# Delta rule in a hybrid encoder block: one head's first phase a piece later, one filler piece moved from step 8 to step 3

## The chip, the cores and the metric

The kernel runs on one core of a Trainium2 chip. The metric is the time of one execution on the device, in microseconds; a kernel's time is the median of several executions. Beside these runs one more execution was taken with the hardware profiler on; all lines of a profile below come from that one.

Engines are named as the profile names them: PE is TensorE (matmuls), PEld its weight loads, DVE is VectorE, ACT is ScalarE, POOL is GpSimd, SP is SyncE, which here issues DMAs. Each engine works through its own queue in order.

## The reference

The reference is one layer of a bidirectional encoder block on 256 tokens of 2048 channels. From a normalized and modulated input it computes one large projection, whose columns feed two branches: an mLSTM (branch A, 4 heads) and a gated delta rule (branch B, 16 heads of 128), each run forwards and backwards over the sequence. Both are projected back, merged by gates and added to the input; a SwiGLU feed-forward part follows. The change touches the schedule of branch B:

```python
qkv = jax.nn.silu(centred_depthwise_conv(b_qkv, gdn_conv_w))
q_b = l2_normalize(heads(b_q, B_HEADS, B_DK)) * (B_DK ** -0.5)
k_b = l2_normalize(heads(b_k, B_HEADS, B_DK))
...
a_mat = jnp.eye(CHUNK) + betac[..., :, None] * jnp.einsum('nbhid,nbhjd->nbhij', kc, kc) * decay_strict
t_mat = lax.linalg.triangular_solve(a_mat, jnp.broadcast_to(jnp.eye(CHUNK), a_mat.shape),
                                    left_side=True, lower=True, unit_diagonal=True)
u = jnp.einsum('nbhij,nbhje->nbhie', t_mat, betac[..., None] * vc)
w = jnp.einsum('nbhij,nbhjd->nbhid', t_mat, (betac * jnp.exp(gc))[..., None] * kc)
...
v_new = u_ - jnp.einsum('bhid,bhde->bhie', w_, s_mem)
o = jnp.einsum('bhid,bhde->bhie', q_ * jnp.exp(g_)[..., None], s_mem) + jnp.einsum('bhij,bhje->bhie', attn, v_new)
s_mem = jnp.exp(g_last) * s_mem + jnp.einsum('bhjd,bhje->bhde', k_ * jnp.exp(g_last - g_), v_new)
```

The modulation (shift, scale, gate) is a matrix-vector product with a weight of 6 x 2048 rows.

## The kernel before

**Heads, groups and pairs.** The 16 delta heads form four groups of four (`GRP = 4`). Each group g goes through an inversion of small triangular blocks (`gdn_invert`, `gdn_blocks`), and then its heads are worked on in two pairs, p = 0 (the "first pair") and p = 1 (the "second pair"), by `gdn_phase2(g, p)`. Phase 2 is a generator of nine steps; each step is a few matmuls and the copies behind them, and each step's matmuls need the copies of the step before. In the trace their PSUM tiles are called p (steps 1 to 4, lines 830, 839, 852 and 864), pa (step 5), pb (step 6), pc (step 7), po (step 8) and px (step 9).

**Pieces between the steps.** So that PE has work while it would wait for a step's copies, pieces of large projections are put between the steps. Those come from `stream(h0)`, line 956: for the two heads h0 and h0+1 of the group after, three jobs `b_job(h, j)` (the columns of k, q and v), each of two pieces. A piece of a `b_job` is 8 blocks of three 128x256 matmuls (the weights are split into a high and a low part: `wh` by ACT, `wl` by DVE), and the last piece of a job ends in `gdn_conv`: ACT copies the result into a padded tile, a depthwise conv follows (one step on ACT, four on DVE, line 351), and a silu on ACT (line 354) writes into kq or vf. That silu is put off (the list `behind`) and emitted with the next job's piece. When the 12 pieces of the two heads are out, `stream` takes further pieces from the list `fills` (other projections).

**Phase 1 inside the stream.** Six pieces after a head's first, all three of its columns are there, and `stream` notes two entries in `todo` for it: the first half of `gdn_phase1(h)` runs behind the second piece from then, its second half behind the fourth. The first half has four scans on DVE, splits of k and q (`kqh`, `kql`), squares (`sqkq`), and on PE two transposes of vf and eight one-column matmuls into `vps`; the second half has six matmuls into two `ks` tiles, some 16 DVE instructions that read them, and DMAs on POOL: four into `inst_d`, one back into `uu` for the next inversion, and `decay_load(h + 2)`. So the pair's first head has its halves behind pieces 8 and 10, and the second behind 14 and 16, where the stream of a pair ends.

**The counts.** The main loop runs steps n = 1 to 9, and behind each step as many pieces as a tuple says: `after` for first pairs, `second` for second pairs of groups 0 to 2, `last` for both pairs of group 3, for which there are no further heads. Counting up `after` gives 1, 3, 4, 6, 8, 10, 12, 16 pieces behind steps 1 to 8, and `second` gives 2, 4, 5, 7, 9, 11, 13, 16. In first pairs, steps 1 to 4 also advance `gdn_blocks`, which copies blocks out of `cg` into X (steps 1 and 2) and UL (steps 3 and 4; line 813 on DVE, line 815 on ACT).

**The modulation rows.** `pump()`, line 159, is called in each piece. It keeps one 1 MB row of the modulation weight in flight (tile `ada`, loaded through SyncE) and, when a row has been there for three calls, emits its product and sum on DVE (line 125). The flag `held` keeps it from doing so in steps 1 to 3 of a pair.

**Order.** The code's order is a priority. A planner in the framework orders each engine's queue by it with a model of times, and can pull an instruction ahead where its model sees the engine free; only what is wrapped in `order(...)` keeps program order on its engine.

Of the kernel before, what the change touches and what calls it, by code (L numbers as in the profile page):

```python
# [25 lines left out]
GRP = 4  # L26
# [26 lines left out]
def hybrid_block(ctx: ExitStack, tc: tile.TileContext, xr, nfr, crow, pk_d, cst_d, ada2, ada4, win0, winb, wint, wba, wbb, wo, wgu, wd, out, dbg=None):  # L53
# [228 lines left out]
    def fill(n=1):  # L282

        while n and fills:
            if next(fills[0], None):
                n -= 1
            else:
                fills.pop(0)
# [103 lines left out]
    def b_job(h, j):  # L392
        return fjob(f"b{h}_{j}", winb[3 * (h - GRP) + j], lambda ps: gdn_conv(h, j, ps))
# [562 lines left out]
    def stream(h0):  # L956

        todo = []

        def piece():  # L960

            for q in list(todo):
                q[0] -= 1
                if not q[0]:
                    todo.remove(q)
                    next(heads1[q[1]])

        for h in range(h0, min(h0 + 2, NH_B)):
            for j in range(3):
                for _ in b_job(h, j):  # L970
                    piece()
                    yield True
            todo += [[2, h], [4, h]]
        while todo:
            fill(1)
            piece()
            yield True
        while True:
            fill(1)
            yield True  # L980
# [94 lines left out]
        yield  # L1075

    heads1 = {h: gdn_phase1(h) for h in range(NH_B)}
    after = (0, 1, 2, 1, 2, 2, 2, 2, 4, 0)
    last = (0, 1, 2, 1, 2, 2, 1, 1, 3, 0)
    second = (0, 2, 2, 1, 2, 2, 2, 2, 3, 0)  # L1080

# [21 lines left out]
    for g in range(4):  # L1103
# [15 lines left out]
        for p in range(2):  # L1119
            pieces = stream(4 * g + 2 * p + 4)  # L1120
            for n in range(1, 10):

                held[0] = n < 4
                if p == 0:
                    next(blocks, None)
                next(pairs[p], None)
                if g == 3 and n == (8, 4)[p]:
                    next(first2[p])
                for _ in range(last[n] if g == 3 else second[n] if p else after[n]):
                    next(pieces)  # L1130
            for _ in pairs[p]:
                pass

            if g < 3:
                while 4 * g + 2 * p + 5 not in heads:
                    next(pieces)
# [577 lines left out]
```

## Time and profile before

| what | value |
|---|---|
| median of 3 runs | 1943.1 us |
| lowest and highest run | 1942.42 and 1946.88 us |
| the profiled execution | 1947.25 us |
| its span from first to last instruction | 1945.5 us |
| granted TensorE clock, mean over the span | 0.998 |

The span is what the profile's shares refer to. In a list of groups or a timeline a line has the start (timeline only), the busy time, the engine, the source line, the operation, and "out<-in" with the names of tiles, then the number of instructions; "[0.76 <-ACT vf L354]" means that the engine stood idle for 0.76 us before it, until ACT finished writing vf at line 354. In a table of stretches, a number in brackets is a count of instructions. Matmuls are pipelined and their ends are modelled: two of them can overlap in the listing.

### The profile page before, as it was taken

To read this page: it belongs to the slowest core of one execution; us is meant where nothing else is said; L and a number is where in the kernel's file an instruction comes from. 1 tells how busy PE (TensorE), PEld (TensorE's weight loads), DVE (VectorE), ACT (ScalarE), POOL (GpSimd) and SP (SyncE) were. 2 spreads that over 40 slices of the span, in tenths; PEclk is the share of its full clock that TensorE was granted. 3 is DMA by queue.
4 is the path that set the end of the run, shared out by engine and by line. 5 is a ranking of instruction groups with operands and counts; after the bars stand their busy time and mean duration, and the time that the engine had idled before them with its cause. 6 is when DMAs were issued, how large, how long until landed. Compare 5 with 4: busy or idle time off the path is not lost.

```text
span 1945.5 us, 27233 instructions
## 1 busy us (share of the span) xinstructions
PE 1916.4 (99%) x10448; PEld 1700.4 (87%) x10448; DVE 1407.1 (72%) x2087; ACT 1028.0 (53%) x1562; POOL 124.1 (6%) x223
## 2 busy tenths in 40 slices
PE   8999999999999999999999999999999999999997
PEld 6888889998999899889788888888888888888886
DVE  6788886888888789866577888766666565555554
ACT  3147646775776587565544445644444444444443
POOL 0001220111011101120100000200000000000000
PEclk9999999999999999999999999999999999999999
DMA  9997676667676766686787898576777665565663
GB/s 398 420 360 243 181 258 249 216 221 238 219 231 205 235 225 238 208 286 244 252 307 262 352 349 321 195 260 244 248 250 252 238 221 204 203 208 203 199 211 131
DMA packets 80772, 485.67 MB, mean 250 GB/s; under 512 B 11433, under 2 KB 17137, under 8 KB 26625
## 3 DMA queue, kind: packets, MB, share of 16 engines
q1 hardware_dynamic: 64368, 451.02, 64.2%
q0 software_dynamic: 8672, 17.88, 4.4%
q10 hardware_dynamic: 7602, 15.03, 2.0%
q8 instruction: 82, 1.34, 0.3%
q14 instruction: 48, 0.39, 0.1%
HBM read 467.07 MB, written 16.82 MB: 249 GB/s over the span
## 4 chain that ended last, share of the span: by engine, by line
PE 86%; DMA 6%; DVE 5%; ACT 2%; issue 1%; POOL 0%; SPq 0%; DVEq 0%; ACTq 0%; POOLq 0%
PE acc_up L247 4%; PE acc_up L248 4%; PE acc_up L249 4%; PE acc_gt L248 4%; PE acc_d L248 4%; PE acc_gt L249 4%; PE acc_d L247 4%; PE acc_d L249 4%; PE acc_gt L247 4%; DMA ra<-ada 3%; PE acc_b L186 3%; PE acc_o L247 3%; PE acc_o L248 3%; PE acc_o L249 3%; PE acc_b L187 3%; PE acc_b L188 3%
## 5 line engine op out<-in xcount | busy, mean ns | idle before, releaser
L215 DVE TENSOR_TENSOR wl_d<-raw_d,wh_d 128x1024 fp32r<-128x1024 f32 x88 | 107.7, 1225 | 105.9 <-ACT wh_d L213 105.9
L215 DVE TENSOR_TENSOR wl_up<-raw_up,wh_up 128x1024 fp32r<-128x1024 f32 x88 | 107.7, 1225 | 100.7 <-ACT wh_up L213 100.7
L215 DVE TENSOR_TENSOR wl_gt<-raw_gt,wh_gt 128x1024 fp32r<-128x1024 f32 x88 | 107.7, 1224 | 76.9 <-ACT wh_gt L213 76.9
L186 PE MATMUL acc_b<-hh,wh_b 128*128 128x256 f32 x576 | 162.0, 281 | 0.0
L213 ACT ACTIVATE wh_d<-raw_d 128x1024 fp32r<-128x1024 f32 x88 | 92.9, 1056 | 126.8 <-PE acc_d L248 118.0
L188 PE MATMUL acc_b<-hh,wl_b 128*128 128x256 f32 x576 | 158.6, 276 | 0.0
L187 PE MATMUL acc_b<-hl,wh_b 128*128 128x256 f32 x576 | 158.5, 275 | 0.0
L213 ACT ACTIVATE wh_gt<-raw_gt 128x1024 fp32r<-128x1024 f32 x88 | 92.9, 1056 | 121.7 <-PE acc_gt L248 75.7
L213 ACT ACTIVATE wh_up<-raw_up 128x1024 fp32r<-128x1024 f32 x88 | 92.8, 1056 | 108.0 <-PE acc_up L248 77.0
L125 DVE SCALAR_TENSOR_TENSOR ada<-ada,crow 128x2048 f32<-128x2048 f32 x64 | 146.3, 2286 | 0.0
L247 PE MATMUL acc_up<-wh_up,hfh 128*128 128x512 f32 x352 | 133.4, 379 | 0.0
L248 PE MATMUL acc_up<-wh_up,hfl 128*128 128x512 f32 x352 | 133.4, 379 | 0.0
L249 PE MATMUL acc_up<-wl_up,hfh 128*128 128x512 f32 x352 | 133.4, 379 | 0.0
L247 PE MATMUL acc_gt<-wh_gt,hfh 128*128 128x512 f32 x344 | 131.6, 383 | 0.0
L248 PE MATMUL acc_gt<-wh_gt,hfl 128*128 128x512 f32 x344 | 130.5, 379 | 0.2 <-DVE hfl L1481 0.2
L248 PE MATMUL acc_d<-wh_d,ffl 128*128 128x512 f32 x344 | 130.5, 379 | 0.0
L249 PE MATMUL acc_gt<-wl_gt,hfh 128*128 128x512 f32 x344 | 130.4, 379 | 0.0
L247 PE MATMUL acc_d<-wh_d,ffh 128*128 128x512 f32 x344 | 130.4, 379 | 0.0
L249 PE MATMUL acc_d<-wl_d,ffh 128*128 128x512 f32 x344 | 130.4, 379 | 0.0
L603 PE MATMUL first<-x,raw 128*128 128x256 f32 x488 | 108.8, 382 | 6.4 <-ACT x L595 6.4
L603 PEld LDWEIGHTS first<-x,raw 128*128 128x128 f32 x488 | 91.6, 190 | 23.6 <-ACT x L595 11.6
L187 PEld LDWEIGHTS acc_b<-hl,wh_b 128*128 128x128 f32 x576 | 110.6, 192 | 0.1
(403 smaller groups left out, 5293.6 us busy)
## 6 DMA issues: line engine op xcount, KB each, us to landing
ada<-ada SPq DMA_DIRECT2D x64, 1024.0 KB, 5.3
raw_gt<-wgu SPq DMA_DIRECT2D x44, 1024.0 KB, 4.9
raw_up<-wgu SPq DMA_DIRECT2D x44, 1024.0 KB, 4.9
raw_d<-wd SPq DMA_DIRECT2D x44, 1024.0 KB, 4.9
raw_b<-winb SPq DMA_DIRECT2D x36, 1024.0 KB, 5.6
ra<-ada SPq DMA_DIRECT2D x30, 1025.0 KB, 15.1
raw_z<-wint SPq DMA_DIRECT2D x16, 1024.0 KB, 4.9
raw_v<-wint SPq DMA_DIRECT2D x16, 1024.0 KB, 5.9
```

Source lines behind the costliest of these rows:

```text
L125: order(V.scalar_tensor_tensor(raw, raw, 1.0, row_c[:, :D], ALU.mult, ALU.mult, accum_out=mod[:, c : c + 1]))
L186: PE.matmul(o, wh[:, k], woven(hh[:, kk]), start=kk == 0, stop=False)
L187: PE.matmul(o, wh[:, k], woven(hl[:, kk]), start=False, stop=False)
L188: PE.matmul(o, wl[:, k], woven(hh[:, kk]), start=False, stop=kk == KB - 1)
L213: order(S.activation(wh, raws[u][:, k0 : k0 + 2], AF.Copy), early)
L215: order(V.tensor_tensor(wl, raws[u][:, k0 : k0 + 2], wh.bitcast(F32), ALU.subtract), early or beside[0])
L247: order(PE.matmul(ps[t], xh[:, kk, c], woven(wh[:, k]), start=kk == 0, stop=False), early and steps > 1)
L248: PE.matmul(ps[t], xl[:, kk, c], woven(wh[:, k]), start=False, stop=False)
L249: PE.matmul(ps[t], xh[:, kk, c], woven(wl[:, k]), start=False, stop=kk == last)
L603: PE.matmul(first[o], raw[:, o], x[:, b], start=b == 0 and o % 2 == 0, stop=b == KB - 1 and o % 2 == 1)
```

## The change

Two tuples and two numbers change. For a head h with h % 4 = 2 (heads 6, 10 and 14: the first head of the stream in the second pairs of groups 0, 1 and 2), both halves of phase 1 run one piece later. In first pairs, two pieces in place of one stand behind step 3, and three in place of four behind step 8. The counts behind the steps of first pairs so become 1, 3, 5, 7, 9, 11, 13, 16.

```diff
@@ -970,7 +970,8 @@
                 for _ in b_job(h, j):
                     piece()
                     yield True
-            todo += [[2, h], [4, h]]
+            late = h % GRP == 2
+            todo += [[2 + late, h], [4 + late, h]]
         while todo:
             fill(1)
             piece()
@@ -1075,7 +1076,7 @@
         yield
 
     heads1 = {h: gdn_phase1(h) for h in range(NH_B)}
-    after = (0, 1, 2, 1, 2, 2, 2, 2, 4, 0)
+    after = (0, 1, 2, 2, 2, 2, 2, 2, 3, 0)
     last = (0, 1, 2, 1, 2, 2, 1, 1, 3, 0)
     second = (0, 2, 2, 1, 2, 2, 2, 2, 3, 0)
 
```

## The prediction

> **What bounds the kernel now.** I read the page first, for the engine that has no slack.
>
> ```profile
> span 1945.5 us, 27233 instructions
> PE 1916.4 (99%) x10448; PEld 1700.4 (87%) x10448; DVE 1407.1 (72%) x2087; ACT 1028.0 (53%) x1562; POOL 124.1 (6%) x223
> ```
>
> TensorE (PE) is busy 99% of the span. The edit adds no instruction and takes none away; it only moves work in time. So it can change the end in one way: by the time in which PE stands idle. I therefore asked for busy times by stretch, one stretch for each of the six pairs that the edit touches (two pairs in each of the groups 0, 1 and 2; lines in this order).
>
> ```profile
> core 0: us, PE busy (x) PEld busy (x) DVE busy (x) ACT busy (x) POOL busy (x), PEclk, DMA share, GB/s
> 314.60:373.00 58.40, 57.50 (x480) 56.11 (x478) 48.72 (x95) 44.13 (x92) 3.56 (x7) 1.00 0.67 221
> 373.00:432.00 59.00, 58.24 (x459) 55.99 (x458) 51.99 (x108) 42.97 (x90) 7.04 (x14) 1.00 0.69 221
> ...
> 494.60:552.10 57.50, 57.28 (x480) 56.07 (x478) 48.71 (x96) 44.27 (x91) 3.55 (x7) 1.00 0.67 228
> 552.10:611.00 58.90, 58.14 (x458) 55.93 (x457) 51.89 (x107) 42.88 (x90) 6.93 (x14) 1.00 0.69 221
> ...
> 672.30:729.70 57.40, 57.18 (x479) 55.93 (x477) 48.27 (x95) 44.95 (x89) 3.59 (x7) 1.00 0.66 218
> 729.70:789.00 59.30, 59.21 (x509) 58.13 (x509) 54.27 (x113) 44.43 (x93) 6.16 (x12) 1.00 0.68 228
> ```
>
> Length less PE's busy time is PE's idle time: 0.90, 0.22 and 0.22 us in the three first pairs, 0.76, 0.76 and 0.09 us in the three second pairs, together 2.95 us. This is all that the edit can win inside these pairs. Which waits these are is told by the list of waits of PE:
>
> ```profile
> engine line waited for: us in total, times, longest us
> ...
> PE acc_z L249 <- DVE wl_z L215: 1.8, 3, 0.7
> PE vps L674 <- ACT vf L354: 1.5, 2, 0.8
> PE acc_mb L249 <- DVE wl_mb L215: 1.3, 1, 1.3
> ...
> PE p L864 <- DVE pt L853: 0.7, 1, 0.7
> PE pb L888 <- DVE r L889: 0.4, 2, 0.2
> ...
> PE pa L877 <- DVE UL L813: 0.2, 1, 0.2
> ```
>
> The two vps waits are those of the second pairs of groups 0 and 1. The p and pa waits belong to the first pair of group 0, the two pb waits to the first pairs of groups 1 and 2. The other two rows lie outside the pairs.
>
> **How long a piece is.** In the second pair of group 1, PE starts a matmul of a projection job every 0.11 us; its modelled duration, 0.28, overlaps the next:
>
> ```profile
> 577.81 0.28 PE L187 MATMUL acc_b<-hl,wh_b 128*128 128x256 f32 x1
> 577.92 0.28 PE L188 MATMUL acc_b<-hh,wl_b 128*128 128x256 f32 x1
> 577.98 0.48 DVE L351 SCALAR_TENSOR_TENSOR cv<-pad,pk,cv 128x256 f32<-128x256 f32 x1
> ...
> 578.37 2.29 DVE L125 SCALAR_TENSOR_TENSOR ada<-ada,crow 128x2048 f32<-128x2048 f32 x1
> 578.49 0.42 ACT L354 ACTIVATE vf<-cv 128x256 f32<-128x256 f32 x1 [1.24 <-DVE cv L351]
> ...
> 578.96 0.44 PE L674 MATMUL vps<-cst,vf 128*128 128x128 f32 x2 [0.76 <-ACT vf L354]
> ```
>
> A b_job piece is 8 blocks of 3 matmuls, so 24 x 0.11 = 2.7 us. The rows also show the vps wait: the last of the four conv steps on VectorE (DVE) starts at 577.98, ScalarE's silu into vf starts at 578.49, and the transposes that read vf start at 578.96, 0.76 us late by the modelled end of the last matmul.
>
> **Part 1: the late head (h = 6, 10, 14).** Its first half (2 transposes and 8 one-column matmuls on PE, kqh and sqkq on ACT, kql and four scans on DVE) moves from behind piece 8 to behind piece 9, its second half from behind piece 10 to behind 11. Order on PE before: pa, piece 8, vps, piece 9, pb, piece 10, ks, piece 11, pc. After: pa, 8, 9, vps, pb, 10, 11, ks, pc. The vps comes 2.7 us later against a vf whose conv is not moved; 0.76 is less than 2.7, so both waits go and the third pair's 0.09 with them: -1.61. The moved second half also issues DMAs on POOL: four into inst_d, the one back into uu, and decay_load of head h+2. POOL is busy 6 to 7 us of 59 in these pairs and nothing is moved past another POOL instruction; uu is read only in the inversion, which still waits for the pair's last head (behind piece 16 as before), and the decay rows of h+2 are read a pair later or more. Cost 0. Without that slack it would be one piece, 2.7 us, each time. The SyncE queue isn't touched by this part.
>
> What is late next is pb, now right behind vps as it is in the first pairs. There its second half waits 0.22 us for r, because VectorE has put an ada row (2.29) in front:
>
> ```profile
> 519.76 2.28 DVE L125 SCALAR_TENSOR_TENSOR ada<-ada,crow 128x2048 f32<-128x2048 f32 x1
> ...
> 523.22 0.42 DVE L889 TENSOR_TENSOR r<-vv,pb 128x256 f32<-128x256 f32 x1
> ...
> 523.70 0.71 PE L888 MATMUL pb<-z,gg 128*128 128x128 f32 x4 [0.22 <-DVE r L889]
> ```
>
> The row can fall there in none or in all three: 0 to 0.66. I take 0.66, since the ada row is given out in the first piece of step 6 in both kinds of pair.
>
> **Part 2: one more piece behind step 3 of first pairs.** Steps 4 to 7 stand one piece later than before against pieces, conv and vps. In group 0 the wait goes that step 4 has for pt:
>
> ```profile
> 325.77 2.29 DVE L125 SCALAR_TENSOR_TENSOR ada<-ada,crow 128x2048 f32<-128x2048 f32 x1
> ...
> 328.38 0.69 DVE L853 TENSOR_TENSOR pt<-p,cst 128x512 f32<-128x512 f32 x1
> ...
> 329.12 0.43 PE L864 MATMUL p<-X,pt 128*128 128x64 f32 x2 [0.70 <-DVE pt L853]
> ```
>
> With 48 matmuls in place of 24, PE would come to step 4 about 2.7 us later, and 0.70 is covered. The pa wait of 0.2 goes likewise, since the UL copies that it waits for don't move. The pb of groups 1 and 2 comes a piece after vps, as in today's second pairs, where it shows no wait. Together -0.90 - 0.22 - 0.22 = -1.34.
>
> The held flag covers steps 1 to 3, so the first ada row is now given out in piece 6, then in 10 and 14, no longer in 5, 9 and 13. That is still three in 16 pieces, so none is left over for later. SyncE issues each ada load one piece later, behind one more raw load at most:
>
> ```profile
> ada<-ada SPq DMA_DIRECT2D x64, 1024.0 KB, 5.3
> ```
>
> From issue to landing takes 5.3 us, and a row's use is three pieces, 8 us, away: cost 0.
>
> What is late next is vf. From step 4 on the first pairs now have today's layout of second pairs: pa, piece 8, vps. And they have more to do there: the UL copies out of cg, which only first pairs have.
>
> ```profile
> 511.69 1.68 ACT L815 ACTIVATE UL<-cg 32x256 f32<-32x256 f32 x4
> ...
> 513.17 1.17 DVE L813 COPY UL<-cg 32x256 f32<-32x256 f32 x4
> ...
> 518.73 0.43 ACT L354 ACTIVATE vf<-cv 128x256 f32<-128x256 f32 x1
> ...
> 520.53 0.38 PE L674 MATMUL vps<-cst,vf 128*128 128x128 f32 x2
> ```
>
> Against pieces, vps itself isn't moved (behind piece 8 in both kernels), and today vf is ready 520.53 - 519.16 = 1.37 us before it. What eats this margin is the ada row, 2.29 us given out a piece later and so right before vf's conv, and the z copies of pa, which come later too. Lower bound of the new wait: 0, if VectorE, which has a backlog anyway, just does the same work in another order. Upper bound: the 0.76 of second pairs plus both copies, 0.76 + 1.17 + 1.68 = 3.6. I take 0.4, half of the second pairs' row, because total work ahead of vf is the same and only its order is worse: 3 x 0.4 = +1.2.
>
> **Part 3: one fewer behind step 8.** Three pieces, 8 us, stay between po and px; second pairs have three today and show no wait at px. Cost 0, and the pair still ends behind 16 pieces.
>
> **Sum.** -1.61 + 0.66 - 1.34 + 1.2 = -1.1 us. The profiled execution took 1947.25 us (span 1945.5), so it would be about 1946.1; that execution lies 4.1 above the median of 1943.1, and I carry the difference to the median: 1942.0.
>
> **The rivals.**
>
> First pairs wait for vf (the slower side). With w for the new wait in each first pair, the total is 3w + 0.66 - 2.95, so from w = 0.76, exactly today's wait of the second pairs, the kernel is slower than before. At the upper bound, 3.6, it is +8.5: 1951.6. For it speaks that the layout is one that waits today; against it the margin of 1.37 us. 0.3% is 5.8 us, about what a measurement of this kernel can tell from no change; that needs w = 2.7.
>
> [...] The trace's one dip in mid-kernel has this length, 3.40 us at 0.50, though PE has no idle time there:
>
> ```profile
> 946.40:949.80 3.40, 3.40 (x5) 1.35 (x4) 0.00 (x0) 1.63 (x2) 0.00 (x0) 0.50 0.98 336
> ```
>
> [...]
>
> All waits go: vf keeps its margin and pb never waits. -2.95, so 1940.1. For it: the margin. Against: in-order VectorE with the ada row in a worse place.
>
> The order doesn't come out as written. Not all instructions are held to program order; the ada row above starts at 578.37, before step 6, in whose first piece it is given out. If the planner puts vps, conv and ada where they were, nothing changes: 1943.1.
>
> Something outside the pairs moves: a planner that shifts by some us may order the inversion or later stages otherwise. The outside waits quoted (1.8 + 1.3), the dip (1.7) and the pairs (2.95) bound a gain at 7.8 us, 1935.3; there is no such bound for a loss.
>
> **How the numbers follow.** Forecast 0.43 (1942.0); vf wait 0.2, of which 0.08 above 5.8 us; all waits go 0.15; order unchanged 0.1; something outside 0.12, of which 0.07 is a gain over 0.3% and 0.05 a loss over it. So faster 0.07, slower 0.08 + 0.05 = 0.13, same 0.80. The range: 1938.8 to 1947.5. Its lower end is "all waits go" less the half microsecond or so by which the runs lie below their median; its upper end is w = 1.7, +2.8, plus some of the 3.8 us by which the highest run shown lies above the median.
>
> **What would show it.** In the changed profile: no vps wait in second pairs and no p L864 wait in the first pair of group 0 (parts 1 and 2 right); vps L674 <- ACT vf in first pairs, its length w (the term I am least sure of); pb L888 <- DVE r up to three times in second pairs; PE idle in the six stretches about 1.9 in place of 2.95. Wrong would be: idle time in a stretch above 3 us, a vps wait left in second pairs, another dip of the clock, or a change that lies outside 314 to 789 us.

## The result, and the profile after

The changed kernel takes 1951.33 us (median of 5 runs, 1950.75 to 1953.38), the kernel before 1943.96 us (5 runs, 1942.42 to 1946.88). The ratio is 1.0035, with a 95% interval of 1.0025 to 1.0046: by the ratio 6.8 us slower (the two medians differ by 7.4), a little over 0.3% and outside the predicted range. The profiled execution took 1953.38 us.

The page's top, after:

```profile
span 1951.5 us, 27218 instructions
PE 1921.3 (98%) x10448; PEld 1706.6 (87%) x10448; DVE 1408.5 (72%) x2087; ACT 1030.5 (53%) x1563; POOL 124.7 (6%) x223
```

PE has the same 10448 matmuls, but its busy time rose by 4.9 us, and ScalarE has one instruction more. Neither should happen in a pure reordering, and both are clues: matmuls took longer, and something was added to ScalarE.

Where the time came from is read by noting when PE starts step 1 (the first matmul of tile p) and step 9 (px) in both traces:

| stretch | before, us | after, us | difference |
|---|---|---|---|
| group 0, first pair (step 1 to step 1 of the second) | 58.31 | 60.12 | +1.81 |
| group 0, second pair (step 1 to step 9) | 57.61 | 57.45 | -0.16 |
| group 1, first pair | 57.41 | 57.39 | -0.02 |
| group 1, second pair | 57.61 | 57.44 | -0.17 |
| group 2, first pair | 57.42 | 58.01 | +0.59 |
| group 2, second pair | 57.42 | 61.48 | +4.06 |

The sum is 6.11 us, and the spans differ by 6.05; the rest of the kernel cancels out. Two places make the loss: the first pair of group 0, and the turn of group 2 from its first to its second pair. The same stretches as busy times (columns as in the prediction; group 0 first pair, group 2 both pairs):

```profile
314.40:374.60 60.20, 59.03 (x480) 57.68 (x478) 48.72 (x95) 44.23 (x92) 3.57 (x7) 0.97 0.63 214
...
673.90:731.90 58.00, 57.48 (x478) 55.88 (x476) 48.06 (x97) 45.63 (x91) 3.58 (x7) 1.00 0.65 229
731.90:795.30 63.40, 60.70 (x508) 59.69 (x509) 55.23 (x112) 46.31 (x95) 6.16 (x12) 0.97 0.63 209
```

Two of them have a granted clock of 0.97. Idle time alone (1.17, 0.52 and 2.70 us here) is less than the loss. PE's list of waits, after:

```profile
PE pb L888 <- DVE r L889: 1.9, 3, 0.8
PE acc_b L188 <- DVE wl_b L183: 1.2, 1, 1.2
...
PE vps L674 <- ACT vf L354: 1.2, 1, 1.2
PE p L839 <- DVE pt L831: 1.1, 1, 1.1
...
PE p L830 <- DVE at L719: 0.4, 1, 0.4
```

The second pairs' vps waits and the waits of step 4 and 5 in group 0 are gone, as forecast. New are a vps wait of 1.2 us in the first pair of group 0, three pb waits in the second pairs, and, in the turn of group 2, where the old kernel had none, waits in steps 1 and 2 and a wait of 1.2 us for wl_b in the piece behind them.

**The turn of group 2.** ScalarE's timeline there, before:

```profile
719.49 1.28 ACT L931 ACT_TABLE_LOAD   x1
720.79 0.30 ACT L931 ACTIVATE so<-so,epsc 128x4 f32<-128x4 f32 x1
720.99 1.04 ACT L181 ACTIVATE wh_a<-raw_a 128x1024 fp32r<-128x1024 f32 x1
722.05 1.28 ACT L368 ACT_TABLE_LOAD   x1
723.34 1.08 ACT L368 ACTIVATE ev_o<-acc_o 128x512 f32<-128x512 f32 x2
724.44 1.28 ACT L686 ACT_TABLE_LOAD   x1
...
725.74 0.26 ACT L686 ACTIVATE nn<-vps,epsc 128x4 f32<-128x4 f32 x1
...
726.55 1.05 ACT L181 ACTIVATE wh_b<-raw_b 128x1024 fp32r<-128x1024 f32 x1
```

And after:

```profile
722.09 1.28 ACT L368 ACT_TABLE_LOAD   x1
723.38 0.60 ACT L368 ACTIVATE ev_o<-acc_o 128x512 f32<-128x512 f32 x1
724.00 1.28 ACT L931 ACT_TABLE_LOAD   x1
725.29 0.30 ACT L931 ACTIVATE so<-so,epsc 128x4 f32<-128x4 f32 x1
725.61 1.28 ACT L368 ACT_TABLE_LOAD   x1
726.90 0.60 ACT L368 ACTIVATE ev_o<-acc_o 128x512 f32<-128x512 f32 x1
727.52 1.28 ACT L686 ACT_TABLE_LOAD   x1
...
728.81 0.26 ACT L686 ACTIVATE nn<-vps,epsc 128x4 f32<-128x4 f32 x1
...
732.82 1.06 ACT L181 ACTIVATE wh_b<-raw_b 128x1024 fp32r<-128x1024 f32 x1 [0.52 <-ACT obt L914]
```

Two filler pieces used to stand between po and the vps of the pair's second head; one does now. The filler there is the end of an output gate job of the mLSTM, whose two evictions are sigmoids. They now become ready while the norm behind po and phase 1 want square roots, and the planner put sigmoid, root, sigmoid, root on ScalarE's queue. Each of the four stands behind a table load of 1.28 us: four loads in place of three. The root nn ends at 729.07, and what hangs on it follows late: VectorE's readers of ks, and behind them in its queue pt, for which step 2 waits. VectorE and PE there, after:

```profile
729.11 0.18 DVE L687 RECIPROCAL sm<-nn 128x4 f32<-128x4 f32 x1 [1.75 <-ACT nn L686]
...
731.43 0.28 DVE L719 TENSOR_TENSOR at<-ks,dec 128x128 f32<-128x128 f32 x1
...
733.23 0.65 DVE L831 TENSOR_TENSOR pt<-p,cst 128x512 f32<-128x512 f32 x1
```

```profile
731.86 1.05 PE L830 MATMUL p<-R,cc 128*128 128x32 f32 x8 [0.44 <-DVE at L719]
734.03 1.05 PE L839 MATMUL p<-R,pt 128*128 128x32 f32 x8 [1.12 <-DVE pt L831]
...
736.59 0.58 PE L188 MATMUL acc_b<-hh,wl_b 128*128 128x256 f32 x1 [1.21 <-DVE wl_b L183]
```

The order of the queues is another there, too. In the old kernel the split wh_b of the next pair's first piece starts at 726.55, ahead of the copies out of px (obt), and 26 matmuls of that piece stand between steps 1 and 2 on PE. In the changed kernel the planner left the split behind those copies, at 732.82, although its data had landed (the last load of raw_b before it lands at 728.78) and ScalarE stood idle for 0.65 and 0.58 us in between, and it put step 2 directly behind step 1, so that no piece covers the wait for pt. The three waits are 0.44 + 1.12 + 1.21 = 2.77 us of the 0.59 + 4.06 = 4.65 that the turn loses.

**The clock.** Stretches of 3.4 us around the two places, after, all columns as before:

```profile
340.20:343.60 3.40, 2.23 (x20) 2.04 (x19) 3.40 (x6) 3.38 (x6) 0.00 (x0) 1.00 0.60 200
343.62:347.03 3.41, 3.41 (x18) 3.41 (x17) 1.84 (x5) 1.58 (x5) 0.00 (x0) 0.50 0.99 411
...
732.73:736.14 3.41, 1.53 (x12) 1.26 (x11) 3.09 (x7) 3.25 (x8) 2.54 (x6) 1.00 0.31 91
736.15:739.56 3.41, 2.97 (x14) 2.97 (x15) 3.14 (x5) 3.28 (x9) 0.92 (x2) 0.50 0.63 73
```

Behind a stretch in which PE worked 2.23 or 1.53 us of 3.4, the clock is at half for 3.41 us. In it PE starts a matmul of a piece every 0.21 us (343.83, 344.05 and 344.26 in the timeline), against 0.11 at full clock. So half of what PE works in that time is lost, by an estimate from these rows: 1.7 us in group 0, and 1.5 us in the turn, where PE is busy for 2.97 us of it. This is where the longer busy time comes from. Half-clock stretches in mid-kernel: one before (at 946), four after (343, 736, 951 and 1016). The last two lie where PE does one-column matmuls for the mLSTM (24 from 948.36 to 951.10 us, 24 from 1012.27 to 1015.00) and come and go between all the runs below (both, one or neither).

Two theories now stand for the loss, and one against this reading of the clock. A: the loss comes from the counts of first pairs, through the table loads in group 2 and the late vf in group 0, each made worse by a half-clock stretch. B: it comes from the late heads and their pb waits. C: half-clock stretches fall by chance.

### The profile page after: what moved, and what is told of

It is laid out like the page before. It is cut to its first block, busy times and chain, and to the rows that moved or that the text cites. A ratio compares the mean times of both kernels' runs of the same rounds, so it can differ in the third digit from the quotient of the medians.

```text
span 1951.5 us, 27218 instructions
## 1 busy us (share of the span) xinstructions
PE 1921.3 (98%) x10448; PEld 1706.6 (87%) x10448; DVE 1408.5 (72%) x2087; ACT 1030.5 (53%) x1563; POOL 124.7 (6%) x223
## 4 chain that ended last, share of the span: by engine, by line
PE 90%; DMA 4%; DVE 4%; ACT 1%; issue 1%; POOL 0%; SPq 0%; DVEq 0%; POOLq 0%; ACTq 0%
PE acc_up L249 4%; PE acc_up L247 4%; PE acc_up L248 4%; PE acc_gt L248 4%; PE acc_d L247 4%; PE acc_gt L249 4%; PE acc_d L249 4%; PE acc_d L248 4%; PE acc_gt L247 4%; DMA ra<-ada 3%; PE acc_b L186 3%; PE acc_b L188 3%; PE acc_b L187 3%; PE acc_o L247 3%; PE acc_o L249 3%; PE acc_o L248 3%
## 5 line engine op out<-in xcount | busy, mean ns | idle before, releaser
L188 PEld LDWEIGHTS acc_b<-hh,wl_b 128*128 128x128 f32 x576 | 112.0, 194 | 1.4 <-DVE wl_b L183 1.4
L186 PEld LDWEIGHTS acc_b<-hh,wh_b 128*128 128x128 f32 x576 | 112.0, 194 | 0.1
```

The lines of the kernel that those rows point to most:

```text
L186: PE.matmul(o, wh[:, k], woven(hh[:, kk]), start=kk == 0, stop=False)
L188: PE.matmul(o, wl[:, k], woven(hh[:, kk]), start=False, stop=kk == KB - 1)
```

## The experiments

Medians and ratios are against runs of the kernel before on the same chip (its median there was 1944.35 to 1945.2 us); 0.1% is 1.9 us.

**1. The late heads alone.**

```diff
-    after = (0, 1, 2, 2, 2, 2, 2, 2, 3, 0)
+    after = (0, 1, 2, 1, 2, 2, 2, 2, 4, 0)
```

(against the changed kernel)

> Only the late heads 6, 10 and 14; the counts behind the steps as before. Theory A (the loss comes from the counts of first pairs: the wait for vf in group 0 and the turn of group 2, each with a halved clock window): about as before, between -1 and +1.5 us, because the second pairs only exchange a vps wait of 0.76 us for a pb wait of 0.7 us. Rival B (the loss comes from the late heads, whose pb waits for r are now 0.7 us in place of nothing): +4 us or more.

1944.34 us, ratio 0.9999 (0.9990 to 1.0008): no change. B falls. The exchange is as stated: its list of PE's waits has no vps, and

```profile
PE pb L888 <- DVE r L889: 2.0, 4, 0.8
```

**2. The new counts alone.**

```diff
-            late = h % GRP == 2
-            todo += [[2 + late, h], [4 + late, h]]
+            todo += [[2, h], [4, h]]
```

> Only the new counts behind the steps of first pairs; no head is late. Theory A: nearly the whole loss, +5 to +8 us, with the vps wait of over 1 us in group 0, the four table loads at the turn of group 2 and two more windows at half clock than before. Rival B: about as before, under +2 us.

1951.37 us, ratio 1.0033 (1.0021 to 1.0045): the whole loss, as A has it. Its profile has half-clock stretches at 342 us and, for two windows of 3.41 us on end, at 734 us. With the waits of steps 1 and 2 as in the changed kernel, the two pairs of group 2 lose 6.1 us in this trace, against 4.65 with one window.

**3. The change, but group 2 keeps the old counts.**

```diff
-                for _ in range(last[n] if g == 3 else second[n] if p else after[n]):
+                for _ in range(last[n] if g == 3 else second[n] if p else (early if g == 2 else after)[n]):
```

(`early` is the old tuple.)

> The changed kernel, but the first pair of group 2 keeps the old counts. Theory A: the turn of group 2 goes back to its time of before (three table loads, no wait in steps 1 and 2), 4.6 us less than the changed kernel, so about +2 to +3 us against before. Rival C (the halved windows fall by chance, whatever waits there are): between +4 and +8 us.

1945.72 us, ratio 1.0007 (0.9998 to 1.0016): some 5.5 us below the changed kernel, so group 2 makes most of the loss. The trace has three table loads at the turn and no wait in steps 1 and 2; the vps wait of group 0 (1.2 us) and the half-clock stretch at 342 us are still there.

**4. One piece from behind step 8 to behind step 7, nothing else.**

```diff
-    after = (0, 1, 2, 1, 2, 2, 2, 2, 4, 0)
+    after = (0, 1, 2, 1, 2, 2, 2, 3, 3, 0)
```

(against the old kernel)

> The old kernel with one piece of first pairs moved from behind step 8 to behind step 7; step 3 keeps one piece and no head is late. Theory A: only the turn of group 2 is hit, by the table loads of ScalarE: +3 to +5 us, and no vps wait in group 0. Rival D (the loss needs the piece behind step 3, by which steps 4 to 7 come later): within 1 us of before.

1951.55 us, ratio 1.0035 (1.0022 to 1.0047), more than A expected. D falls: the piece behind step 8 does it alone, with four table loads, the same waits in steps 1 and 2 as the changed kernel, and two half-clock windows in a row from 732.7 us. The first pair of group 0 has no wait for vf, and the second has the same as before.

**5. A copy in place of the sigmoid.** The edit changes the function of two evictions and nothing else: it takes table loads away and leaves the work and the counts as they are.

```diff
-            keep((v_d, o_d)[i][h], (AF.Copy, AF.Sigmoid)[i], f"{'vo'[i]}{h}"),
+            keep((v_d, o_d)[i][h], (AF.Copy, AF.Sigmoid)[i and h != 2], f"{'vo'[i]}{h}"),
```

> The changed kernel, with a plain copy in place of the sigmoid in the eviction of the third mLSTM head's output gate (that sigmoid is left out). All instructions keep their order on every engine; ScalarE has one table load at the turn of group 2 in place of four. Theory A (table loads hold up the turn): the waits of p in steps 1 and 2 of the second pair and the half-clock window there go, 4 to 5 us less than the changed kernel, so +1.5 to +3 us against before. Rival E (the turn is late because of the order of VectorE's work, tables or not): +5 us or more.

1944.85 us, ratio 1.0004 (0.9995 to 1.0012): 0.8 us above before, less than expected. ScalarE at the turn, in this run:

```profile
720.52 0.60 ACT L368 ACTIVATE ev_o<-acc_o 128x512 f32<-128x512 f32 x1 [0.52 <-PE acc_o L249]
721.13 1.28 ACT L931 ACT_TABLE_LOAD   x1
722.43 0.30 ACT L931 ACTIVATE so<-so,epsc 128x4 f32<-128x4 f32 x1
722.63 0.58 ACT L368 ACTIVATE ev_o<-acc_o 128x512 f32<-128x512 f32 x1
723.11 0.26 ACT L686 ACTIVATE nn<-vps,epsc 128x4 f32<-128x4 f32 x1
```

From the first eviction's start to nn's are 2.6 us, against 728.81 - 723.38 = 5.4 in the changed kernel, and the load ahead of that eviction is gone too. The waits in steps 1 and 2 and the one for wl_b vanish from the list. E falls: without the loads the turn isn't late. But the expectation was wrong in one thing. The instructions keep their order only up to nn. Behind it three wh_b splits, the first at 724.13, come ahead of the copies out of px, and 48 matmuls of pieces stand between steps 1 and 2, where the changed kernel has none. So the loads cause the late turn, together with the order that the planner makes around them; how much of the 4.65 us is the loads' own time and how much that order is not shown, here or in run 6.

This run shows a second thing. The vps wait of group 0 is still there (1.17 us, up to 340.88), with its eight one-column matmuls, but no half-clock stretch follows. The four half-clock stretches of the changed kernel begin at 343.62, 736.15, 951.19 and 1016.04 us, which is 115, 63 and 19 steps of 3.413 us apart. Counted on in such steps, which is an estimate, one ends inside the wait in this run's trace, at 340.69 (columns as before):

```profile
337.28:340.69 3.41, 2.43 (x22) 2.24 (x21) 3.34 (x6) 3.41 (x9) 0.00 (x0) 1.00 0.60 252
340.69:344.10 3.41, 3.22 (x29) 3.23 (x30) 3.41 (x5) 3.38 (x7) 0.00 (x0) 1.00 1.03 339
```

Most of the wait lies in the first row and the small matmuls in the second, and the first pair of group 0 takes 58.49 us, 0.2 above before, in place of 60.12. The wait itself only takes the place of the 0.90 us of waits that went. So what that pair loses in the changed kernel is the half-clock window. Why it comes in one trace and not in the other is not shown; that it depends on where the wait falls among the steps is a reading that fits both traces, and by it so much of C is right.

**6. The fillers reordered.** The same test with everything computed.

```diff
+        if i == 2:
+            rest += [m_job(1, i)] + last[0] + [a_vo(1, i)] + last[1]
+            continue
         rest += [m_job(1, i), a_vo(1, i)] + (last[0] + last[1] if i else last[1] + last[0])
```

> The changed kernel, with the list of filler jobs reordered in one place: the third head's four q and k jobs (plain copies at their ends) come before its output gate job (sigmoid at its end), so that no sigmoid falls into the turn of group 2. Everything is computed. Theory A: like the run with the plain copy, +1 to +3 us against before; what is left is the vps wait of group 0 with its half-clock window. Rival E: +5 us or more.

1944.7 us, ratio 1.0002 (0.9992 to 1.0012), 0.4 us above before and a little less than A expected. One table load at the turn, no wait in steps 1 and 2. The half-clock stretch of group 0 is there, at 342.7 us. What is left in this run's list of PE's waits is what A says, and a vps wait of 0.4 us in the second pair of group 2:

```profile
PE vps L677 <- ACT vf L354: 1.6, 2, 1.2
PE pb L891 <- DVE r L892: 1.5, 2, 0.8
```

**7. Extra matmuls inside the waits.** The changed kernel gets work for PE in the waits of group 0 and of the turn (`dense(o, n)` issues n matmuls of 128x256 into a tile that is overwritten):

```diff
         vps = gps(f"vps{h}")
+        if h == 4:
+            dense(vps[:, 0:256], 12)
...
         p1 = gps(f"p1_{g}_{p}")
+        if (g, p) == (2, 1):
+            dense(p1[:, 0:256], 6)
...
         p2 = gps(f"p2_{g}_{p}")
+        if (g, p) == (2, 1):
+            dense(p2[:, 0:256], 12)
```

> The changed kernel, with 12 extra 128x256 matmuls ahead of the vps of head 4, 6 ahead of step 1 and 12 ahead of step 2 of group 2's second pair; their results are overwritten, so nothing else changes. They add 30 x 0.11 = 3.4 us of matmuls, nearly all inside waits of 1.3, 0.6 and 1.3 us. Theory F (a half-clock window follows a window in which PE worked little): the half-clock windows near 343 and 736 us go, and the time falls by 1.7 us for each, less some 0.3 us for matmuls that stick out: 2 to 3 us less than the changed kernel. Rival C (half-clock windows fall by chance or have another cause): the same time as the changed kernel or up to 1 us more, and the windows stay.

1947.44 us, ratio 1.0014 (1.0005 to 1.0022), so about 4 us less than the changed kernel, although 30 matmuls were added and the table loads are all there. C falls for these two places: no half-clock stretch between 24 and 1938 us, and the two critical stretches of this run at full clock:

```profile
340.20:343.60 3.40, 3.40 (x32) 3.38 (x31) 3.40 (x4) 3.35 (x6) 0.00 (x0) 1.00 0.82 270
...
732.60:736.00 3.40, 2.19 (x19) 2.00 (x19) 2.90 (x5) 3.30 (x7) 1.74 (x4) 1.00 0.41 57
```

Two half-clock windows are worth some 3.2 us; the rest of the gain I can't assign. The second row says one thing more: PE is busy for 2.19 us there, less than the 2.23 of the changed kernel at 340.20, and no half-clock stretch follows. Most of its 19 matmuls have 256 columns and none has one, and the other stretch has eight of one column among its 20. PE's busy time alone doesn't decide.

**8 and 9. Narrow and wide matmuls, and the clock.** The old kernel with 64 extra matmuls ahead of step 3 in one pair, of one column and of 256 columns (the second edit replaces the last line of the first):

```diff
         p3 = gps(f"p3_{g}_{p}")
+        if (g, p) == (1, 1):
+            for i in range(64):
+                PE.matmul(p3[:, 256 + i : 257 + i], ident, ones1, start=True, stop=True)
```

```diff
+                PE.matmul(p3[:, 256:512], hh[:, 0, 0:P], woven(hh[:, 1]), start=True, stop=True)
```

> The old kernel with 64 extra one-column matmuls ahead of step 3 of group 1's second pair (each some 0.11 us, 7.2 us in all; their results aren't used). Theory F (a half-clock window of 3.4 us follows a window in which PE worked little, whatever its busy time says): a half-clock window or two begin in or right behind the extra matmuls, and the time is 1.7 us or more above that of the run with 64 wide matmuls. Rival C: no such window, and the two runs take the same time, +7 us against before.

> The control: the old kernel with 64 extra 128x256 matmuls in the same place (each some 0.11 us). Theory F: no half-clock window there; +6 to +7.5 us against before, at least 1.7 us less than the run with one-column matmuls. Rival C: as the run with one-column matmuls.

Wide: 1952.29 us, ratio 1.0036 (1.0024 to 1.0049), +7.1 us as expected, with the clock at 1.00 around the extra matmuls (560 to 572 us). One-column: 1971.84 us, ratio 1.0133 (1.0118 to 1.0149), +26.6 us. My 7.2 us for these was wrong by a factor of two, since each of these matmuls, which are in full precision, is two instructions in the trace (x128 for 64). The view of tile p in the one-column run groups them (shortest, median and longest in ns, then from when to when):

```profile
L852 PE MATMUL p<-ones,cst x128: 169/352/353, 564.9 to 588.3; 128*128 128x1 f32 x128
```

At full clock 37 of them go by in 3.75 us (the first row below), at half clock 95 in 19.80 us (the second), so 128 are 13 us at full clock; the half clock, 23.9 us of it, adds 12, and the sum of 25 lies within the interval (23 to 29 us). The stretches of that run, columns as before, the extra matmuls beginning at 564.85:

```profile
564.85:568.60 3.75, 3.75 (x37) 3.75 (x35) 2.94 (x3) 3.04 (x5) 0.00 (x0) 1.00 0.60 200
568.70:588.50 19.80, 19.80 (x95) 19.80 (x95) 0.00 (x0) 0.00 (x0) 0.00 (x0) 0.50 0.19 74
588.50:592.50 4.00, 4.00 (x19) 4.00 (x20) 1.97 (x3) 0.00 (x0) 0.00 (x0) 0.50 0.00 0
592.60:596.00 3.40, 3.40 (x32) 3.40 (x32) 2.23 (x5) 1.81 (x4) 0.00 (x0) 1.00 0.00 0
```

PE is never idle, yet the clock halves 3.8 us after the first one-column matmul and is back at 1.00 only at 592.60, behind the last one-column matmul (588.3), the eight of 64 columns of step 3 (588.5 to 590.1) and some 2 us of wide ones. So idle time isn't what brought the half clock here: it came with one-column matmuls, of which eight stand behind each vps too, and not with the wide ones of the control. That they are in full precision, unlike the wide ones, is not enough for it. In the old kernel PE does nothing but full-precision matmuls of 256 columns (line 603, 257 in the trace) from 60 to 120 us, and the clock there is 1.00. How much narrow work or idle time it takes, no run here shows.

**10. All first heads late, with the reordered fillers.**

```diff
-            late = h % GRP == 2
+            late = h % 2 == 0
```

> The run with reordered fillers, and the first head of every pair (not only of second pairs) with its first phase a piece later. Theory A with its second half (the vps wait of group 0 comes from a vf that is late by 1.3 us): no vps wait in first pairs, no half-clock window near 343 us, 2 to 3 us less than the run with reordered fillers: -1.5 to +0.5 us against before. Rival: the waits only pass on to pb, and the time stays at that of the run with reordered fillers.

1943.36 us, ratio 0.9991 (0.9982 to 0.9999). The vps wait of group 0 and its half-clock stretch are gone, and this is the only run whose interval lies wholly below 1: 1.8 us faster than the old kernel, if that. Part of the gain passes to pb, as the rival had it. From this run's list of PE's waits:

```profile
PE pb L891 <- DVE r L892: 2.4, 3, 0.9
PE acc_a L188 <- DVE wl_a L183: 1.5, 1, 1.5
```

**11. Modulation rows held back in step 6 as well,** on top of run 10.

```diff
-                held[0] = n < 4
+                held[0] = n < 4 or n == 6
```

> The run with reordered fillers and all first heads late, with modulation rows also held back during step 6, so that VectorE gets r ahead of the 2.3 us row. Theory G (the pb waits come from the row in front of r): the pb waits of 0.9 to 1.0 us shrink to 0.2 us, and the time falls by 2 to 3 us against the run without the hold, -3 to -5 us against before. Rival: the row comes to stand in front of another instruction that PE waits for, and the time stays within 1 us.

1946.99 us, ratio 1.0013 (1.0004 to 1.0022): slower, a miss. VectorE now gets both r ahead of the row, but the pb waits only shrink to 2.0 us over five, and PE waits elsewhere (wl_a 2.2 us, wl_mb 1.2 us). In group 0 r now starts at 345.10, directly behind four conv steps of 2.04 us that VectorE has put in the row's place.

**12. The old kernel with the reordered fillers alone.** The edit is that of run 6.

> The old kernel with the reordered fillers alone. Theory A: the old kernel's turn of group 2 has three table loads but hardly a wait, so there is little to win: -1.5 to +0.5 us. If it is 3 us faster or more, the gain of the later runs comes from the order of the fillers elsewhere and not from the turn.

1946.19 us, ratio 0.9999 (0.9990 to 1.0008): nothing, as expected. So the order of the fillers brings nothing by itself; it matters where the counts bring the sigmoids to the roots.

## Why the prediction was wrong

**Part 3, one fewer behind step 8: this step failed.** It was put at 0, because second pairs have three pieces there and show no wait at px. That looked at how long the stretch is, and not at what fills it: it named neither the filler job that ends there nor the function its eviction runs, and the wait did not come at px but at the two steps behind it. In groups 0 and 1 no wait appears behind it: the second pairs there took 0.16 and 0.17 us less than before, and the first pair of group 1 took 0.02 us less. In group 2 it cost 4.65 us in the trace, and 6.8 us by itself in run 4: four table loads in place of three, the waits of 2.77 us, and one half-clock window or two. The rows that warn of it were in the profile of before: three table loads of 1.28 us within 6.2 us, from 719.49 to 725.72.

**The clock: not in the sum.** The prediction starts from the premise that the edit can change the end only by PE's idle time. That failed: PE's busy time rose by 4.9 us. No term of the forecast is for the clock; the dip's 1.7 us, in the bound for what lies outside the pairs, is half of the 3.40 us at 0.50 in its row. The longest waits in the old kernel's pairs, 0.70 and 0.76 us, left the clock at 1.00. In the changed kernel a wait of 1.17 us, with eight one-column matmuls behind it, was followed by 3.41 us at 0.50 (run 7 takes the window away by filling that wait; in run 5 the clock stays at 1.00 behind the same wait). The row that could have told this was quoted: the dip of the old kernel at 946.4 with PE never idle. 24 one-column matmuls run from 942.94 to 945.68, right before it; in run 8 such matmuls alone bring 23.9 us at half clock, and the wide ones of run 9 bring none.

**Part 2, w: right in sum by luck.** Forecast 3 x 0.4 us; measured 1.17 us in group 0 and under 0.1 us in groups 1 and 2. The mechanism was right: in all three pairs the margin is gone, and the transposes start 0.05 us behind vf. Its size was a guess. In group 0 the last conv step on VectorE ends 0.29 us before vf starts, and vf stands behind kqh and sqkq on ScalarE as well, so most of the wait is VectorE's. The timelines of the changed kernel (start, duration, instruction):

```profile
340.31 0.48 DVE L351 SCALAR_TENSOR_TENSOR cv<-pad,pk,cv 128x256 f32<-128x256 f32 x1
...
340.04 0.64 ACT L668 ACTIVATE kqh<-kq 128x512 fp32r<-128x512 f32 x1
340.56 0.64 ACT L671 ACTIVATE sqkq<-kq 128x512 f32<-128x512 f32 x1
341.08 0.43 ACT L354 ACTIVATE vf<-cv 128x256 f32<-128x256 f32 x1
```

The waits of step 4 and 5 in group 0 went, and the first pairs' pb waits too, as stated. With its half-clock window (1.7) the first pair of group 0 lost 1.8 us all the same. Why VectorE is later in group 0 than in the other groups stays open.

**Part 1: right, one term too small.** The vps waits of second pairs went (-1.6 us), and pb took their place with 1.9 us in place of 0.66; run 1 shows the exchange as a wash. VectorE has more than the ada row in front of r (in the second pair of group 0 a wl_b split and three conv steps as well), so the wait is 0.77 us and not 0.22. The order came out nearly as written in the pairs, so that rival had nothing in it; nor had "all waits go", and runs 10 and 11 show how hard pb's wait is to remove. The lower end of the range was mis-added: 1940.1 less half a microsecond is about 1939.5, not 1938.8; nothing hangs on it.

The rival on the slower side had the right engine, ScalarE, and bounds that hold the measured loss, but the wrong place: vf in all first pairs, not the tables in one turn.

## What to carry to other kernels

Before moving filler work, list what each filler ends in, on every engine it touches: here sigmoids and roots came to alternate on ScalarE and brought four table loads of 1.28 us in place of three, in one instance of a loop and not in the others. A PE wait should be priced with what lies around it: here a wait of 1.2 us with eight tiny matmuls behind it cost 0.2 us net in one trace and 1.8 us in another, by whether a half-clock window followed. If a wait can't be removed, running wide dummy matmuls inside it can be worth more than it costs, as in run 7 (30 matmuls added, ratio 1.0014 in place of 1.0035). And where a planner orders the queues, look at what it did with the order before a wait is put down to one engine.

## What the runs showed of the hardware that was not expected

In these traces the matmul clock fell to 0.50 for 3.41 us at a time: in the changed kernel from 343.62 to 347.03 us, behind a stretch of 3.40 us with a wait of 1.17 us and eight one-column matmuls, and from 736.15 to 739.56 us, behind one of 3.41 us in which PE was busy for 1.53. It did so also where PE was busy all the time by the trace: 128 one-column matmuls in a row (run 8) brought 23.9 us at half clock, seven times 3.41, and 64 matmuls of 256 columns in the same place (run 9) none. Behind the same wait of 1.17 us with the same eight matmuls the clock stayed at 1.00 in run 5. What else decides, these runs leave open.
